# A rope kernel: sin in another PSUM bank than cos, the last tile stored whole, other small transfers between loads and stores

## The chip, the cores and the metric

One core of one Trainium2 chip. The metric is the device time of one execution in microseconds (us). The kernel before takes 162.44 us (median of 3 runs, 162.35 to 162.64). A profiled execution of it has a span of 160.7 us from the first to the last instruction. A profile gives busy times of the engines (PE = TensorE, DVE = VectorE, ACT = ScalarE, POOL = GpSimd, SP = the engine that issues the transfers here), and a record of each DMA packet: start, duration, bytes.

Four terms are used throughout. PSUM is the memory that matmuls write to, divided into banks. A ring is the queue of packets of one of the sixteen DMA engines; it is free when its packets are done. A landing mark is the 4-byte packet that ends a transfer's share on one engine. A packet is in flight from its start to its end. A run counts as slow when it is over 1.5% above the fastest run of the same kernel; ratios use fast runs alone.

## The reference

Rope multiplies the two halves of each head with tables of cosines and sines and adds them crosswise:

```python
x = x.reshape(16, 512, 16, 64)             # batch, seq, heads, head_dim; float32
x1, x2 = x[..., :32], x[..., 32:]
cos, sin = cos[None, :, None, :], sin[None, :, None, :]    # each (512, 32) before
out = concatenate([x1 * cos - x2 * sin, x1 * sin + x2 * cos], axis=-1)
```

x and out are 33.55 MB each. Nothing is read twice, so 67.1 MB have to move.

## The kernel before

The work is cut into eight tiles of 128 partitions x 8 rows of 1024 floats (4 MiB, 32 KB a partition). Five tile buffers are filled ahead; a tile is changed in place and stored from the same buffer. The three places that the change touches:

```python
FIRST = (3, 8)
LAST_OUT = (4, 8)              # rows at which the last tile's stores are cut
EXTRA = (2, 4, 5, 6)           # partitions of the small transfers
...
    load(0, 0, FIRST[0])
    tabs = bp.tile([P, 2 * dim], FP32, name="b")
    nc.sync.dma_start(out=sin_sb, in_=sin_v)
    nc.sync.dma_start(out=cos_sb, in_=cos_v)
    ...                        # the rest of tile 0, then tiles 1 to 4
    spare = fixed.tile([16, len(EXTRA), 16], FP32)
    for i, n in enumerate(EXTRA):
        nc.sync.dma_start(out=spare[:n, i], in_=sin_v[:n, :16])   # read by nobody
...
    tab = pfix.tile([P, BANK], FP32)                   # one PSUM bank
    cos_t = tab[:, : KK * half]
    sin_t = tab[:, KK * half : 2 * KK * half]          # the same bank
    ...
    nc.tensor.matmul(out=sin_t, lhsT=spread, rhs=sin_sb, start=True, stop=True)   # L113
    nc.tensor.matmul(out=cos_t, lhsT=spread, rhs=cos_sb, start=True, stop=True)   # L114
    nc.vector.tensor_scalar_mul(out=sns[:, :, 0, :], in0=sin_k, scalar1=-1.0)     # L116
    nc.vector.tensor_copy(out=sns[:, :, 1, :], in_=sin_k)                         # L117
```

In the loop over tiles, POOL makes x times sin (L165), VectorE makes x times cos in PSUM (L141) and adds the two (L189); for two of eight rows TensorE and ScalarE do the adding. At the end of each tile SP issues its store (L78); after the store of tile 2 it issues the loads of tiles 5 to 7 (L74), each when the store that used its buffer has landed.

## Time and profile before

| what, in the profiled run of before | value |
|---|---|
| span; time of this run | 160.7 us; 162.47 us |
| last landing marks of the sixteen engines start | 158.45 to 159.51 us (mean 158.79) |
| last pair sum of VectorE ends | 148.23 us |
| landing of the last store | 159.85 us |

The prediction below shows the lines that carry this, and puts the span together from the packet records. One view more is needed, the issuer's own part of the timeline (start, duration, engine and line, transfer, count; the duration of a merged row includes the waits between):

```profile
7.26 6.85 SPq L92 DMA_DIRECT2D spare<-in_sin_dram  x4
30.43 34.26 SPq L78 DMA_DIRECT2D out_dram<-xt  x3
64.86 17.66 SPq L74 DMA_DIRECT2D xt<-in_x_dram  x3
82.63 65.97 SPq L78 DMA_DIRECT2D out_dram<-xt  x6
```

```profile
146.11 2.48 SPq L78 DMA_DIRECT2D out_dram<-xt  x2
```

```profile
148.26 0.33 SPq L78 DMA_DIRECT2D out_dram<-xt  x1
```

These are the first answer for the whole span, then two closer looks at its end. The reader is to see that the second half of the last tile is issued at 148.26, when store 6 is just leaving the rings (148.72 to 149.79 by the landing marks). The first half, issued at 146.11, lies in between and keeps the rings full.

### The profile page before, as it was taken

The numbers are of one execution on the slowest core, as the hardware profiler recorded it, in microseconds if no ns is written. First come the engines' busy times: TensorE is split into PE (matmuls) and PEld (weight loads), VectorE is DVE, ScalarE is ACT, GpSimd is POOL, SyncE is SP. The second block draws the span as 40 slices with busy tenths as digits, with TensorE's granted clock in tenths as the row PEclk, the third lists the DMA queues.
The fourth block names the chain that finished last, engine by engine and source line by source line (L and its number), as shares of the span: only waits on it lengthen the run. The fifth ranks groups of instructions, "written<-read, shape, count | busy, mean of one in ns | idle before, by whom it ended". The sixth has DMA issues, their size and how long they took to land.

```text
span 160.7 us, 443 instructions
## 1 busy us (share of the span) xinstructions
PE 60.8 (38%) x71; PEld 19.3 (12%) x71; DVE 136.3 (85%) x85; ACT 18.7 (12%) x25; POOL 127.1 (79%) x38
## 2 busy tenths in 40 slices
PE   3041925056503931192308350664048402932000
PEld 0011301021102210131003010210022001300000
DVE  1059969999999999999999999999999999998000
ACT  0001311003000301012100310031003010211000
POOL 1039999999999999988998899898998899840000
PEclk9999995557655685559555855576556855595555
DMA  5999999999999999999999999999999999999994
GB/s 177 410 408 473 392 514 400 392 473 440 392 449 449 408 400 498 408 392 498 418 392 465 440 400 465 440 400 408 457 432 408 465 424 408 473 416 416 428 412 204
DMA packets 2787, 67.25 MB, mean 419 GB/s; under 512 B 354, under 2 KB 482, under 8 KB 482
## 3 DMA queue, kind: packets, MB, share of 16 engines
q1 hardware_dynamic: 2786, 67.24, 98.0%
q14 instruction: 1, 0.01, 0.0%
HBM read 33.69 MB, written 33.55 MB: 418 GB/s over the span
## 4 chain that ended last, share of the span: by engine, by line
DVE 68%; issue 12%; POOL 6%; DMA 4%; PE 1%; SPq 0%; DVEq 0%
DVE xt L189 33%; DVE pd L141 31%; POOL b L165 6%; DMA b<-in_sin_dram 4%; DVE pe_ps L141 3%; PE tab L113 1%; PE tab L114 1%; DVE sns L116 0%; DVE xt L150 0%; DVE own_ps L141 0%; SPq L74 0%; DVE sns L117 0%; DVEq L189 0%
## 5 line engine op out<-in xcount | busy, mean ns | idle before, releaser
L165 POOL TENSOR_TENSOR b<-xt,sns 128x2048 f32<-128x2048 f32 (+1 forms) x32 | 126.4, 3978 | 14.7 <-DVE sns L117 9.3
L189 DVE TENSOR_TENSOR xt<-pd,b 128x2048 f32<-128x2048 f32 x24 | 54.9, 2286 | 2.4 <-POOL b L165 1.6
L141 DVE TENSOR_TENSOR pd<-xt,tab 128x2048 f32<-128x2048 f32 x24 | 55.0, 2291 | 0.2
L176 PE MATMUL own_ps<-xt,ident 128*128 128x512 f32 x32 | 30.2, 1100 | 54.4 <-DVE xt L150 48.7
L176 PE MATMUL pe_ps<-b,ident 128*128 128x512 f32 x32 | 28.8, 1001 | 24.0 <-DVE pe_ps L141 24.0
L176 PEld LDWEIGHTS own_ps<-xt,ident 128*128 128x128 f32 x32 | 9.4, 323 | 74.3 <-DVE xt L150 59.7
L209 ACT COPY xt<-own_ps 128x1024 f32<-128x1024 f32 x8 | 8.1, 1012 | 73.7 <-PE own_ps L176 73.7
L181 ACT COPY xt<-pe_ps 128x512 f32<-128x512 f32 x16 | 9.4, 585 | 38.2 <-PE pe_ps L176 38.2
L176 PEld LDWEIGHTS pe_ps<-b,ident 128*128 128x128 f32 x32 | 8.4, 290 | 42.8 <-DVE pe_ps L141 34.1
L141 DVE TENSOR_TENSOR pe_ps<-xt,tab 128x512 f32<-128x512 f32 x16 | 11.0, 685 | 0.0
L141 DVE TENSOR_TENSOR own_ps<-xt,tab 128x1024 f32<-128x1024 f32 x8 | 9.8, 1223 | 0.0
L150 DVE TENSOR_TENSOR xt<-xt,tab 128x1024 f32<-128x1024 f32 x8 | 9.7, 1213 | 0.0
L116 DVE TENSOR_SCALAR sns<-tab 128x256 f32<-128x256 f32 x1 | 0.4, 424 | 8.2 <-PE tab L114 8.2
L113 PE MATMUL tab<-b,spread 64*128 64x256 f32 x2 | 1.2, 697 | 5.0 <-DMA b<-in_sin_dram 5.0
L209 ACT ACT_TABLE_LOAD x1 | 1.3, 1283 | 15.4 <-DVE xt L150 15.4
L101 PE MATMUL own_ps<-zero 128*128 128x512 bf16 x2 | 1.0, 618 | 1.2 <-DVE zero L97 1.2
L113 PEld LDWEIGHTS tab<-b,spread 64*128 64x128 f32 x2 | 0.5, 310 | 5.9 <-issue 5.9
L114 PE MATMUL tab<-b,spread 64*128 64x256 f32 x2 | 1.1, 631 | 0.0
L97 DVE MEMSET zero<- 128x256 uint32 x1 | 0.3, 272 | 0.9 <-PEq L240 0.9
L114 PEld LDWEIGHTS tab<-b,spread 64*128 64x128 f32 x2 | 0.7, 334 | 0.2
L101 PE MATMUL pe_ps<-zero 128*128 128x512 bf16 x1 | 0.6, 631 | 0.0
L101 PEld LDWEIGHTS <-zero 128*128 128x128 bf16 x3 | 0.3, 123 | 1.5 <-DVE zero L97 1.2
(9 smaller groups left out, 1.8 us busy)
## 6 DMA issues: line engine op xcount, KB each, us to landing
xt<-in_x_dram SPq DMA_DIRECT2D x7, 4096.0 KB, 29.8
out_dram<-xt SPq DMA_DIRECT2D x7, 4096.0 KB, 24.7
out_dram<-xt SPq DMA_DIRECT2D x2, 2048.0 KB, 10.2
xt<-in_x_dram SPq DMA_DIRECT2D x1, 2560.0 KB
xt<-in_x_dram SPq DMA_DIRECT2D x1, 1536.0 KB
b<-in_sin_dram SPq DMA_DIRECT2D x1, 64.0 KB
b<-in_cos_dram SPq DMA_DIRECT2D x1, 64.0 KB
spare<-in_sin_dram SPq DMA_DIRECT2D x1, 0.1 KB
```

The source lines that it names most:

```text
L97: nc.vector.memset(zero, 0.0)
L101: nc.tensor.matmul(out=ps, lhsT=zero[:, :P], rhs=zero, start=True, stop=True)
L113: nc.tensor.matmul(out=sin_t, lhsT=spread, rhs=sin_sb, start=True, stop=True)
L114: nc.tensor.matmul(out=cos_t, lhsT=spread, rhs=cos_sb, start=True, stop=True)
L116: nc.vector.tensor_scalar_mul(out=sns[:, :, 0, :], in0=sin_k, scalar1=-1.0)
L141: nc.vector.tensor_tensor(out=o, in0=i, in1=cb, op=ALU.mult)
L150: nc.vector.tensor_tensor(out=heads(r), in0=heads(r), in1=s, op=ALU.mult)
L165: nc.gpsimd.tensor_tensor(out=o, in0=i, in1=sb, op=ALU.mult)
L176: nc.tensor.matmul(out=ps, lhsT=ident, rhs=other, start=False, stop=True, skip_group_check=True)
L181: nc.scalar.copy(out=r, in_=pe_ps)
L189: nc.vector.tensor_tensor(out=r, in0=ps, in1=b, op=ALU.add)
L209: nc.scalar.copy(out=r0, in_=own_ps)
```

## The change

The intent: let VectorE's first use of sin start without waiting for cos, so that all computing runs a little earlier; store the last tile with fewer, larger packets, since its store can now be issued early enough; and use less of the small transfers that sit between loads and stores.

```diff
-LAST_OUT = (4, 8)
-
-EXTRA = (2, 4, 5, 6)
+LAST_OUT = (8,)
+
+EXTRA = (1, 1, 1, 1, 3)
@@
-    sin_t = tab[:, KK * half : 2 * KK * half]
+    sin_t = pd.tile([P, 2 * dim], FP32, name="pd")[:, : KK * half]
```

## The prediction

> **What bounds the kernel now.** I read the page's header and the forty slices first, then the DMA queues, then the chain that ended last, then the waits of the DMA queue, and last the packet records of the trace (start, duration and bytes of each packet; they name no DMA engine).
>
> ```profile
> span 160.7 us, 443 instructions
> ...
> DVE  1059969999999999999999999999999999998000
> ...
> DMA  5999999999999999999999999999999999999994
> ...
> q1 hardware_dynamic: 2786, 67.24, 98.0%
> ...
> HBM read 33.69 MB, written 33.55 MB: 418 GB/s over the span
> ...
> DVE 68%; issue 12%; POOL 6%; DMA 4%; PE 1%; SPq 0%; DVEq 0%
> ```
>
> The reader is to see two rows that both look full. VectorE is at 9 almost everywhere, but its last three slices (12 us) are 0; the DMA row is at 9 up to the last slice, and its queue's packets took 98.0% of sixteen engines' span. The chain gives VectorE 68%, because it follows the last instruction back and the last instruction is VectorE's; it doesn't say that a faster VectorE would end the kernel sooner. The 12% of "issue" is the stretch after VectorE has stopped, in which stores drain. A table of stretches says it more sharply:
>
> ```profile
> core 0: us, PE busy (x) PEld busy (x) DVE busy (x) ACT busy (x) POOL busy (x), PEclk, DMA share, GB/s
> ...
> 60.00:100.00 40.00, 15.25 (x18) 4.56 (x16) 39.69 (x24) 4.95 (x7) 37.73 (x11) 0.59 1.00 433
> 100.00:147.00 47.00, 21.27 (x24) 6.37 (x24) 46.52 (x29) 6.55 (x9) 39.69 (x10) 0.61 1.01 432
> ...
> 149.80:158.40 8.60, 0.00 (x0) 0.00 (x0) 0.00 (x0) 0.00 (x0) 0.00 (x0) 0.50 1.00 429
> ```
>
> The DMA share is 1.00 with VectorE busy and with VectorE silent; the rate is the same 429 to 433 GB/s. The packet records agree: a 32 KB packet takes 1.213 us (median of 1792, and the fastest 25% too), a 16 KB packet 0.611 us (256 of them). Sixteen packets are in flight in every microsecond from 3 us to 158 us, but for one at 79 us (15.8). The first packet starts at 1.75 us, and the packets' summed time over 16 is 157.46 us. 1.75 + 157.46 = 159.2 us, and the sixteen last packets end between 158.45 and 159.51 us. So the span is: 1.75 us before the first byte, 157.0 us of solid transfers, 0.7 us in which the engines that ended early wait for the last one (mean end 158.79, last 159.51), and 1.2 us of landing and closing. Nothing that computes is in that sum, provided that the queue never runs dry.
>
> **What the Trainium skill says.** (1) "DMA: Bandwidth & Descriptors", section "Where 436 GB/s comes from": the ceiling of the ports is 435.2 GB/s. The trace agrees: 16 x 32768 B / 1.213 us = 432 GB/s. The same section expects about 358 GB/s for traffic with HBM; here the whole span averages 418, so the measurement decides against that figure. (2) The same page, "Why a DMA increments its semaphore by 16 and not by 1": the number of engines k is the largest up to 16 that divides the slowest dimension that isn't 1, and on this path the lowest-numbered k engines are used. The trace agrees for the small transfers of before: 17 packets of 64 B, which is 2+4+5+6, and 337 of 4 B, which is 20 large transfers x 16 + 17. For a transfer of one partition the slowest dimension that isn't 1 could be the 16 elements, which would make k = 16 with 4 B each; no run here shows it yet. (3) "PSUM — Partial Sum Buffer", section "PSUM bank collisions raise a hardware error": engines must be kept apart by bank, not by address. The trace agrees that VectorE's read of sin waits for the matmul of cos, which writes other columns of the same bank.
>
> ```profile
> 7.68 1.19 PE tab L113 x2
> 8.87 0.87 PE tab L114 x2
> 9.74 0.02 issue
> 9.76 0.42 DVE sns L116
> 10.19 0.34 DVE sns L117
> 10.53 0.07 issue
> 10.60 3.30 POOL b L165
> ```
>
> This is the chain in order of time. L113 spreads sin and is done at 8.87; L114 spreads cos and is done at 9.74; VectorE's first use of sin starts 20 ns after L114, 0.89 us after its own data are there. POOL, which waited 9.3 us for the tables, starts at 10.60.
>
> **The change part by part.** *Sin in another bank.* sin_t moves from columns 256 to 511 of the cos bank to the buffer of the pair products, whose first real use comes later on the same VectorE queue. Removed: the 0.87 us of L114 ahead of L116. Nothing is added. POOL then starts at about 9.73, and because the first pair sum at 21.94 waits for POOL (1.6 us) and VectorE is then back to back, everything that VectorE does after it moves by 0.87: the last pair sum ends at 147.37 instead of 148.23. cos is needed by VectorE only after the two sign copies and the 0.23 us copy, at about 9.95, after L114's 9.74, so it becomes no new wait. What this is worth by itself: the stores of tiles 0 to 6 are issued into a queue that has work for many microseconds (store 0 issued at 30.43 behind loads that end at 51.8; store 6 issued at 132.25, its first packets after 139.0), so 0.0 us. It matters only for the last store.
>
> *Last tile whole.* Before, the two halves are issued at 146.11 and 148.26; store 6 leaves the engines between 148.72 and 149.79. After, one store is issued when the last pair sum ends, at about 147.40. How long from issue to the first packets? The first load has an idle queue: issued at 0.73, sixteen packets in flight between 1.75 and 2.36, so 1.0 to 1.6 us (the page in (2) gives about 0.6 us to the first byte; this case shows 1.0, and I use that). 147.40 + 1.0 to 1.6 = 148.4 to 149.0, against rings that come free from 148.72 to 149.79. So no gap on most engines and at most 0.3 us on the earliest, which end 1 us ahead of the last anyway. Gain: on one engine a tile in whole rows takes 9.681 us (from landing marks at 71.125 and 80.806), in two halves 4.862 + 4.862 = 9.724, so 0.043 us less. The two parts belong together: without the 0.87 us, the packets would come at 149.3 to 149.9 and nearly every engine would idle 0.1 to 0.6 us.
>
> *Small transfers.* They lie between the loads, which end at 51.8, and store 0. Data plus mark take 13 ns of an engine (starts 51.794, 51.802, 51.807). Before, engines 0 and 1 have four, 2 and 3 three, 4 two, 5 one. After, with k as many engines as partitions, engine 0 has five, 1 and 2 one, the others none: +13 ns on engine 0, up to -39 ns on the others. If one partition is cut into sixteen pieces, every engine has four more pairs than engines 6 to 15 have now, +52 ns at most. There are five in place of four, so the rotation of the eight landing semaphores moves by one: store 0 would wait for load 2's landing at about 33.3 rather than go at 29.6, still 18 us before its ring position is reached; the later ones wait for stores that landed 50 us earlier. Nothing on the path.
>
> Sum: 0 - 0.043 + (-0.04 to +0.05) = about -0.04 us, plus luck in the order in which engines end.
>
> **The rivals.** *The last store comes too late.* If the issue of 128 rows under load takes 2 us instead of 1.0 to 1.6, packets come at 149.4 to 150.0, later than every ring is free: end + 0.2 us. For it: nobody waits on an idle ring under load in this trace, so the latency is known from the cold start alone. Against: even then the loss is bounded by a few tenths. If the 0.87 us isn't gained as well, it is up to 1 us, 163.4. *The compute path carries to the end.* If VectorE's chain set the end, 0.87 us would come off: 161.6. Against it: the rings held sixteen packets in flight while VectorE worked, and 10 us of stores follow it. *The engines' order of ending changes.* The spread of the sixteen marks is 0.51 us at 22.6, 0.55 at 61.4, 0.80 at 80.8, 0.86 at 100.2, 1.06 at 110 and stays there; it grows where single packets took 1.25 to 1.62 us (at 50.5, 80.0 and 108.6 to 109.5). Those slow packets belong to no store or load that the change touches. If the new offsets avoid some of them, up to 0.7 us (159.51 to the mean 158.79) could be won; if they add one on the last engine, 0.4 lost. This is the largest uncertain term.
>
> **Range and chances.** Time and span of the profiled run are 162.47 and 160.7, and the three runs lie in 162.35 to 162.64. From 162.44 I take 0.04 by count and another 0.1 because small offsets were presumably chosen for a better order of ending: 162.3 us. The range 161.9 to 162.7 holds the order of ending (some 0.4 either way) and the small late-store rival. A change of 2% is 3.2 us; the removable parts of the span, the 0.7 us of spread and the 0.043, don't reach it, and the worst rival loses 1 us. Faster by over 2%: 0.01; within 2%: 0.98; slower: 0.01.
>
> **What would show it right or wrong.** In the changed profile: VectorE's first use of sin at about 8.9 us, released by L113 (bank step); POOL's first product at about 9.7 and the last pair sum ending at about 147.4 (shift carried); one last store of 4096 KB issued at about 147.4; still about sixteen packets in flight between 148 and 150 us (no gap), and a mean DMA share of 98%; the number of packets under 512 B telling k for one partition (7 small ones, or 64 and 3). Wrong would be a last pair sum still at 148.2, a hole in the DMA row at 148 to 150, or an end that moves by more than 0.5 us without a change in the spread of the last packets.

## The result

Changed kernel: 162.59 us median (162.23 to 162.75, 6 runs). Before, with the runs on the same occasion: 162.54 us (162.27 to 162.85, 6 runs). The ratio is 0.9999, with a 95% interval of 0.9982 to 1.0016. A ratio is the mean time of one kernel's fast runs over that of the other's of the same rounds, so not quite the ratio of the medians quoted. So the change is worth nothing that the runs can tell.

The page of the changed kernel:

```profile
span 160.8 us, 444 instructions
...
DVE  1079979999999999999999999999999999996000
...
DMA  5999999999999999999999999999999999999993
...
q1 hardware_dynamic: 2622, 67.24, 97.9%
...
DVE 67%; issue 12%; DMA 7%; POOL 4%; SPq 1%; DVEq 0%
```

VectorE stops a little earlier (its last busy slice is 6 instead of 8). The DMA row is what it was: 9 throughout, 97.9% of sixteen engines' span instead of 98.0%. There are 164 packets fewer (2622 instead of 2786): 128 data packets and 16 landing marks of the store that was cut in two, and 10 + 10 of the small transfers.

The timeline of the changed kernel at the start:

```profile
7.82 1.19 PE L113 MATMUL pd<-b,spread 64*128 64x256 f32 x2 [5.17 <-DMA b<-in_sin_dram]
...
8.80 1.06 PE L114 MATMUL tab<-b,spread 64*128 64x256 f32 x2
9.04 0.42 DVE L116 TENSOR_SCALAR sns<-pd 128x256 f32<-128x256 f32 x1 [7.49 <-PE pd L113]
9.38 0.41 DVE L117 COPY sns<-pd 128x256 f32<-128x256 f32 x1
9.88 4.51 POOL L165 TENSOR_TENSOR b<-xt,sns 128x2048 f32<-128x2048 f32 x1 [8.57 <-DVE sns L117]
```

The brackets say how long an engine idled and what released it. L116 now starts at 9.04, released by L113 (before: 9.76, released by L114), while the matmul of cos is still running (8.80 + 1.06 = 9.86). POOL starts at 9.88 instead of 10.60. Both moved by 0.72 us and not by 0.87, because sin itself landed later in this execution: L113 starts at 7.82 instead of 7.68.

The end of the changed kernel, VectorE's last instruction and then the issue of the last store, from two looks at the timeline:

```profile
145.21 2.29 DVE L189 TENSOR_TENSOR xt<-pd,b 128x2048 f32<-128x2048 f32 x1
147.56 0.33 SPq L78 DMA_DIRECT2D out_dram<-xt  x1
```

The last pair sum ends at 147.50 instead of 148.23: the 0.73 us of the start have arrived at the end undiminished. The one store of 4096 KB is issued at 147.56. Store 6 leaves the rings between 148.75 and 149.95, and the packets of store 7 follow each mark 5 or 6 ns later; there are 16.0 packets or more in flight in every microsecond from 140 to 158. So all computing ended 0.73 us earlier, and the transfers went on as before. The sixteen last marks lie between 158.43 and 159.63 us, mean 158.75 (before 158.79), last one 0.12 us later than before.

### The profile page after: what moved, and what is told of

Its sections match the earlier page's. It is cut to its first block, busy times and chain, and to the rows that moved or that the text cites. A ratio compares the mean times of both kernels' runs of the same rounds, so it can differ in the third digit from the quotient of the medians.

```text
span 160.8 us, 444 instructions
## 1 busy us (share of the span) xinstructions
PE 55.9 (35%) x71; PEld 18.4 (11%) x71; DVE 136.2 (85%) x85; ACT 18.4 (11%) x25; POOL 127.1 (79%) x38
## 3 DMA queue, kind: packets, MB, share of 16 engines
q1 hardware_dynamic: 2622, 67.24, 97.9%
## 4 chain that ended last, share of the span: by engine, by line
DVE 67%; issue 12%; DMA 7%; POOL 4%; SPq 1%; DVEq 0%
DVE xt L189 33%; DVE pd L141 30%; DMA xt<-in_x_dram 7%; POOL b L165 4%; DVE pe_ps L141 4%; SPq L85 0%; SPq L84 0%; DVE own_ps L141 0%; DVE xt L150 0%; DMA spare<-in_sin_dram 0%; SPq L74 0%; DVEq L189 0%
## 5 line engine op out<-in xcount | busy, mean ns | idle before, releaser
L176 PE MATMUL own_ps<-xt,ident 128*128 128x512 f32 x32 | 29.2, 1068 | 57.0 <-DVE xt L150 52.1
L176 PE MATMUL pe_ps<-b,ident 128*128 128x512 f32 x32 | 24.6, 863 | 25.8 <-DVE pe_ps L141 23.3
L176 PEld LDWEIGHTS pe_ps<-b,ident 128*128 128x128 f32 x32 | 7.5, 260 | 43.4 <-DVE pe_ps L141 35.4
L116 DVE TENSOR_SCALAR sns<-pd 128x256 f32<-128x256 f32 x1 | 0.4, 424 | 7.5 <-PE pd L113 7.5
L113 PE MATMUL pd<-b,spread 64*128 64x256 f32 x2 | 1.2, 696 | 5.2 <-DMA b<-in_sin_dram 5.2
L113 PEld LDWEIGHTS pd<-b,spread 64*128 64x128 f32 x2 | 0.5, 306 | 6.0 <-issue 6.0
L114 PE MATMUL tab<-b,spread 64*128 64x256 f32 x2 | 1.1, 631 | 0.0
L114 PEld LDWEIGHTS tab<-b,spread 64*128 64x128 f32 x2 | 0.7, 333 | 0.2
```

Of the source, the lines that this page charges most:

```text
L176: nc.tensor.matmul(out=ps, lhsT=ident, rhs=other, start=False, stop=True, skip_group_check=True)
```

## The experiments

All runs are of one core; those of one group shared a chip and the runs of the kernel before. Packets in flight and marks are from the packet records. The summary first:

| run | edit | median us (runs) | before, same chip | ratio to before, 95% interval |
|---|---|---|---|---|
| e1_bank | before + sin in its bank | 162.65 (5) | 162.74 | 0.9993, 0.9979 to 1.0007 |
| e2_whole | before + last store whole | 162.77 (6) | 162.74 | 0.9998, 0.9983 to 1.0013 |
| e3_small | before + new small transfers | 162.57 (6) | 162.74 | 0.9992, 0.9974 to 1.0009 |
| e4_none | changed, no small transfers | 162.45 (5) | 162.74 | 0.9983, 0.9970 to 0.9996 |
| e5_late | changed, last store later | 163.34 (4, one of them slow) | 162.34 | 1.0057, 1.0040 to 1.0074 |
| e6_light | changed, less VectorE work | 162.34 (4) | 162.34 | 1.0001, 0.9985 to 1.0018 |
| e7_bytes | changed + 512 KB of load | 163.70 (4) | 162.34 | 1.0088, 1.0070 to 1.0106 |
| e8_eight | changed, eight small transfers | 166.07 (4) | 162.34 | 1.0233, 1.0217 to 1.0248 |
| e9_late2 | e5_late once more | 163.29 (4) | 162.31 | 1.0053, 1.0016 to 1.0089 |
| e10_late4 | changed, still later | 165.83 (4) | 162.31 | 1.0206, 1.0175 to 1.0237 |
| e11_none2 | e4_none once more | 162.30 (6) | 162.31 | 0.9987, 0.9963 to 1.0012 |
| e12_after | changed kernel once more | 162.40 (6) | 162.31 | 0.9994, 0.9968 to 1.0020 |

The theory throughout: sixteen DMA engines, each at a fixed pace, set the end from 1.75 us on, and computing is hidden as long as no ring runs dry. The main rival at first: the parts have effects that cancel.

### The three parts one at a time

e1_bank:

```diff
-    sin_t = tab[:, KK * half : 2 * KK * half]
+    sin_t = pd.tile([P, 2 * dim], FP32, name="pd")[:, : KK * half]
```

> The kernel before with the bank part alone. Theory (the sixteen DMA engines set the end, computing is hidden): last pair sum ends 0.7 to 0.9 us earlier, at about 147.4, sixteen packets in flight as before, time the same as before within 0.2 us. Rival (VectorE's chain carries to the end): 0.7 to 0.9 us faster.

Measured: the same time. The timeline of this run shows that the part worked:

```profile
7.67 1.19 PE L113 MATMUL pd<-b,spread 64*128 64x256 f32 x2 [5.03 <-DMA b<-in_sin_dram]
...
8.90 0.42 DVE L116 TENSOR_SCALAR sns<-pd 128x256 f32<-128x256 f32 x1 [7.35 <-PE pd L113]
...
9.74 4.51 POOL L165 TENSOR_TENSOR b<-xt,sns 128x2048 f32<-128x2048 f32 x1 [8.44 <-DVE sns L117]
```

With sin landing at the same moment as before, L116 moves by 0.86 us (9.76 to 8.90) and the last pair sum ends at 147.38, 0.85 us before that of the kernel before. The time did not follow: 0.85 us would be a ratio of 0.9948, outside the interval. VectorE's chain doesn't set the end.

e2_whole:

```diff
-LAST_OUT = (4, 8)
+LAST_OUT = (8,)
```

> The kernel before with the whole last store alone, which is then issued at about 148.3 instead of 147.6. Theory: packets in 1.0 to 1.2 us for the first engine and up to 1.6 for the last, so rings that come free at 148.7 wait some 0.5 us, the last one (149.8) hardly: last packet 0 to 0.15 us later, time within 0.2 us of before, and a dip below sixteen packets in flight between 148.7 and 149.9. Rival (issue under load takes 2 us): 0.5 to 0.7 us slower. Rival (the two parts of the change cancel, whole store gains): faster by more than 0.2 us.

Measured: the same time. Without the bank part the last store is issued here at 148.09:

```profile
148.09 0.33 SPq L78 DMA_DIRECT2D out_dram<-xt  x1
```

The rings come free from 148.58 on; the first packets of the store start between 148.92 and 149.12 on fourteen of them. The other two, free at 149.43 and 150.20, had theirs waiting. So up to fourteen rings stood idle, for up to 0.34 us, and 11.7 packets were in flight in the half microsecond from 148.5. But the end did not move by that: the ring that came free last, at 150.20, ended last, at 159.88, 9.68 us later. The dip filled time in which the early engines would have waited at the end (marks' spread 1.62 us before the dip, 1.21 us after it). It also measured the term that the prediction had from a cold start only: from issue to packets 0.83 to 1.03 us.

e3_small:

```diff
-EXTRA = (2, 4, 5, 6)
+EXTRA = (1, 1, 1, 1, 3)
```

> The kernel before with the new small transfers alone. Theory: 13 ns of an engine each, time the same within 0.2 us. Store 0 issued at about 33.4 instead of 30.4 because of the shifted semaphore rotation, with no gap in the packets. Rival (offsets of engines matter for the order of ending): spread of the last sixteen packets clearly different from 1.06 us in the direction of the time.

Measured: the same time. Store 0 is issued at 33.38, without a gap in the packets, since the loads end at 51.9. The spread of the last marks is 1.32 us (before 1.06), and the time is not longer for it: the spread is that of one execution, and the times of one kernel differ by 0.6 us among its runs (before: 162.36 to 162.96).

So the parts don't cancel: each by itself does nothing that the runs can tell, within about 0.2%.

### No small transfers

```diff
-    for i, n in enumerate(EXTRA):
-        nc.sync.dma_start(out=spare[:n, i], in_=sin_v[:n, :16])
```

> The changed kernel with no small transfers at all. Theory: 0.01 to 0.07 us less work on engine 0, time the same within 0.2 us, spread of the last packets again 0.8 to 1.2 us, because it grows at single slow packets and not at the small transfers. Rival (the small transfers steer the order of ending): spread below 0.5 us or above 1.6, time moved with it by 0.3 us or more.

Measured: 162.45, ratio 0.9983, just clear of 1, and 0.28 us below before by the ratio: a miss of my 0.2, if a small one. The spread of its last marks was 1.04 us, no other than with the transfers. Since this was a candidate for a better kernel, it ran again beside the changed kernel:

> The changed kernel without small transfers, once more on another occasion, beside the changed kernel itself: it came out at 0.9983 of before, just clear of 1. Theory (chance in the order of ending): within 0.15 us of before and of the changed kernel this time. Rival (a real gain): again 0.2 to 0.3 us faster than both.

> The changed kernel itself, as the partner of the run without small transfers. Theory: within 0.2 us of before; spread of the sixteen last packets 0.8 to 1.5 us as in the other runs.

Measured on another chip: 162.30 without them, 162.40 with them (means 162.29 and 162.40), 162.31 before; the ratio to before is 0.9987 and its interval holds 1. Spreads 0.89 and 1.07 us. Both occasions lean the same way, but the second is not clear of chance: without them it is 0.11 us under the changed kernel, and 0.18 us under before by the means, of which 0.12 us come from one run of before at 163.67. Whether the small transfers cost a tenth of a microsecond stays open; that they gain anything, no run shows.

### Less computing, more bytes

e6_light leaves VectorE's in-place product out (a wrong result):

```diff
-        own_product(r0)
```

> The changed kernel without VectorE's in-place product of the own row (wrong result on purpose): 8 x 1.2 us less on VectorE. Theory: VectorE and all issues of stores run some us ahead, time the same within 0.2 us. Rival (VectorE bounds): 5 to 9 us faster.

Measured: ratio 1.0001 to before. Eight products of 1.21 us are gone, and the last store is issued 4.5 us earlier than in the changed kernel (line from the issuer's timeline):

```profile
143.01 0.33 SPq L78 DMA_DIRECT2D out_dram<-xt  x1
```

It isn't 9.7 us earlier because computing now meets POOL and the loads: in this run POOL waited 3.3 us and VectorE 1.4 us for loads. The time doesn't change.

e7_bytes:

```diff
+    more = fixed.tile([P, dim], FP32)
+    nc.sync.dma_start(out=more, in_=x_v[0][:, :dim])
```

> The changed kernel with one more load of 512 KB into a buffer that nobody reads, queued after the small transfers. Theory: 524288 B / 432 GB/s = 1.21 us slower, 0.75%, with packets in flight at sixteen all along. Rival (the DMA engines have room): no change.

Measured: 163.70 against 162.34, ratio 1.0088, so 1.4 us by the ratio and 1.36 by the medians (expected 1.21; its marks' mean ends at 159.99, 1.24 us after the 158.75 of the changed kernel's first profile). Taking away ten microseconds of VectorE's work gives nothing; adding 0.8% of bytes costs 0.9% of time. That is what a bound looks like from both sides. The queue's line of this run, packets, MB and share of sixteen engines' span, shows that the engines stayed as full as before:

```profile
q1 hardware_dynamic: 2766, 67.77, 98.1%
```

The 128 added packets of 4 KB took 0.161 us each (median), 1.31 us an engine, which is a little more than 1.21 at the pace of the 32 KB packets.

### How late may the last store be?

e5_late (and the same kernel again as e9_late2) puts two products that nobody reads ahead of the last pair sum; e10_late4 puts four:

```diff
+        if t + 1 == NT:
+            for _ in range(2):          # e10_late4: range(4)
+                cos_product(own_ps, rows(t, ROW_OWN), ROW_OWN)
         pair_sum(*p1, b1)
```

> The changed kernel with two more 128x1024 products on VectorE (to a buffer that nobody reads any more) ahead of the last pair sum: the last store is issued some 2.3 us later, at about 149.85. Theory: the rings are free from 148.7 to 150.0, packets come 1.0 to 1.6 us after the issue, at 150.9 to 151.5, last packet at about 161.1: 1.2 to 1.6 us slower than the changed kernel, with a hole in the DMA row near 150. Rival (the compute chain never matters within a few us): no change. Rival (VectorE's chain sets the end already): 2.3 us slower.

Measured: three of four runs at 163.16 to 163.36 us (ratio of the fast runs 1.0057), about 1.0 us over before, a miss of my 1.2 to 1.6. The fourth run, the one that was profiled, took 192.13 us and counts as slow:

```profile
L176 PE MATMUL pe_ps<-b,ident 128*128 128x512 f32 x32 | 55.9, 1868 | 11.2 <-DVE pe_ps L141 11.2
L176 PE MATMUL own_ps<-xt,ident 128*128 128x512 f32 x32 | 55.5, 1976 | 43.5 <-DVE xt L150 38.6 <-issue 5.0
```

These are groups of instructions (busy us, mean ns of one). TensorE's matmuls took 1.87 and 1.98 us there, against 0.86 and 1.07 us in the changed kernel's profile, VectorE then waited 3.5 us a tile for ScalarE, and the rings ran dry. Why TensorE was slow in that one execution, the profile doesn't show (it gives a granted clock of 1.0, and 0.64 for the changed kernel's, so a lower clock it was not). Nothing about the change is concluded from it. So the same kernel ran again:

> The same kernel as in the run with two more VectorE products ahead of the last pair sum, once more, since that run's profile fell in a slow state. The whole store alone showed 0.83 to 1.03 us from issue to packets on rings that stand idle. With that: issue at about 149.8, packets at 150.6 to 150.9, last packet at about 160.5, some 0.9 us slower than the changed kernel, an idle stretch of all sixteen between about 149.9 and 150.6. Rival (latency of 1.0 to 1.6 us as in the prediction): 1.2 to 1.6 us.

> Four more products in place of two, so 2.3 us more on VectorE before the last store. Theory (once the rings have run dry, the last store's issue sets the end, microsecond for microsecond): 2.2 to 2.4 us slower than with two, 3.1 to 3.3 us slower than the changed kernel. Rival (part of the delay is still hidden): clearly under 2 us more than with two.

Measured: 163.29 and 165.83 us; the changed kernel on the same chip 162.40. Two products cost 0.9 us, as expected, and four 3.4 us, 2.54 more than two: a little over the 2.2 to 2.4 and 3.1 to 3.3 expected. The profiles give the reason. The issues of the last store, first with two products, then with four:

```profile
149.28 0.33 SPq L78 DMA_DIRECT2D out_dram<-xt  x1
```

```profile
152.09 0.33 SPq L78 DMA_DIRECT2D out_dram<-xt  x1
```

The stretches around it, with four products:

```profile
core 0: us, PE busy (x) PEld busy (x) DVE busy (x) ACT busy (x) POOL busy (x), PEclk, DMA share, GB/s
...
148.40:149.90 1.50, 0.00 (x0) 0.00 (x0) 1.47 (x3) 0.00 (x0) 0.00 (x0) 0.50 0.06 22
149.90:152.60 2.70, 0.00 (x0) 0.00 (x0) 2.12 (x1) 0.00 (x0) 0.00 (x0) 0.50 0.00 0
152.60:154.00 1.40, 0.00 (x0) 0.00 (x0) 0.00 (x0) 0.00 (x0) 0.00 (x0) 0.50 0.87 374
```

The next to last number is the DMA share: VectorE is at work for 2.12 us of a stretch in which no DMA engine has anything to do (a packet counts where it starts, so 0.06 in the line above is the tail of packets that began before). The packets start at 150.11 to 150.26 and at 152.92 to 153.06, in both cases 0.83 us after the issue for the first and 0.97 to 0.98 for the last engine. Between the two runs the issue moves by 2.81 us and the last mark by 2.80 us (160.01 to 162.82): once the rings are dry, the issue of the last store sets the end, microsecond for microsecond. That was the theory; the rival, that part of the delay stays hidden, is out. Of the 2.81 us, 2.5 are the two products more (I had put 2.3), and the rest is that sin's matmul (L113) began 0.27 us later in the second of these executions. In the first, the issue came at 149.28 and not at 149.8 as expected; that run was the fastest of its four (163.00).

With 0.83 us, measured on idle rings, the changed kernel's margin can be estimated: its last store is issued at 147.56, so packets are there from 148.39, and the first ring comes free at 148.75. It had 0.36 us to spare before any engine would wait, and over 1 us before the last one would (149.95 less 147.56 + 1.03).

### Eight small transfers

```diff
-EXTRA = (1, 1, 1, 1, 3)
+EXTRA = (1,) * 8
```

> The changed kernel with eight small transfers of one partition in place of five. They cost 13 ns each, but the eighth takes the landing semaphore of load 4, the last load of the first group, and the DMA queue's issuer waits for it until about 52.8; store 0 is issued after that, at about 53. Theory: the rings, which end the loads and small transfers at 51.9 to 52.3, get store 0 only at about 54, so all sixteen stand still for about 1.8 us: 1.5 to 2.2 us slower. Rival (only bytes and packets count): the same within 0.2 us.

Measured: 166.07 us, ratio 1.0233: slower by over 2%, and about twice what I expected. The gap is there as expected, in the issuer's timeline and in the stretches:

```profile
7.03 45.66 SPq L92 DMA_DIRECT2D spare<-in_sin_dram  x8
52.82 10.84 SPq L78 DMA_DIRECT2D out_dram<-xt  x3
```

```profile
core 0: us, PE busy (x) PEld busy (x) DVE busy (x) ACT busy (x) POOL busy (x), PEclk, DMA share, GB/s
...
51.50:52.00 0.50, 0.50 (x2) 0.34 (x1) 0.50 (x2) 0.00 (x0) 0.50 (x1) 0.50 0.04 1
52.00:53.50 1.50, 1.50 (x3) 0.42 (x2) 1.50 (x2) 0.00 (x0) 1.50 (x2) 0.50 0.00 0
```

The eighth small transfer holds the issuer until 52.8, and store 0, finished by VectorE 23 us before, goes out behind it. The rings are empty from 52.0 to about 53.7, and each stands idle for 2.0 us on average. Three small transfers more cost that. What I had not expected is a further 1.5 us: the packets' summed time over 16 is 158.86 us against 157.35 in the changed kernel. After the gap 74 packets of 32 KB take over 1.24 us, 29 us too long in all; the changed kernel has 11 such packets with 1.3 us. Fifteen of the 74 follow the restart directly, but they make up only 0.5 us. The loss lies in 54 packets of up to 2.31 us at 78 to 85 and at 110 to 113 us, where stores and loads take turns. The mean of the last marks is 3.52 us later, which is 2.0 of gap and 1.5 of slow packets.

Why those packets are slow is open. My reading was that engines in step disturb one another, since all sixteen start within 0.2 us of each other after the gap. Step alone is not enough: in e9_late2 and e10_late4 all sixteen restart within 0.15 us of each other for the last store, and none of its packets takes over 1.26 us. Nor does it seem to be needed: the slow profile of e5_late has 27 such packets, 14 us too long, at 112 to 116 us, with marks 1.04 us apart just before.

## Why the prediction was right

**The bound.** Right. The span was put together from 1.75 us of start, transfers without a gap, the last engine's lateness and the landing, and neither 0.85 us less on the compute path (e1_bank) nor 4.5 us (e6_light) moved the time, while 0.8% more bytes did (e7_bytes). Which part of the way, the engines, the ports or the memory, sets the 1.213 us of a 32 KB packet, no run here separates.

**The bank part.** Right: L116 waits for L113 alone, POOL and VectorE run earlier by that much to the very end, 0.85 us where sin landed at the same moment, 0.73 in the changed kernel's profile. The sum gave it 0.0 us of time, and that is what e1_bank measured within its interval. Behind it stood another limit close by: in the changed kernel the chain goes back from POOL's second product, at 14.37 us, to transfers (tile 0's second part, until 13.95, and a small one) and no longer to sin. It costs nothing yet, as POOL's first product ends only then. Three readings in the prediction were wrong without changing its result. The 12% of "issue" are not the stretch after VectorE has stopped: they are 19.0 us of short pieces between VectorE's instructions (0.44 and 0.98 us, again and again), and the chain ends with VectorE at 148.23. Cos does become a new wait: the 0.23 us copy (L119) writes into the cos bank, and in e1_bank it starts at 9.76, just after L114's end at 9.72 and 0.1 us after L117's end (in e5_late, where TensorE was slow, the waits name L114 for it, with 0.9 us); VectorE waits 1.5 us for POOL later, so nothing comes of it. And the pair sum at 21.94 is the second one; the first, at 15.29, doesn't wait.

**The last tile whole.** The 0.043 us are there on each ring: from mark to mark a ring takes 9.681 us for the whole tile (148.746 to 158.427), as computed. The mean of the last marks went from 158.79 to 158.75, which agrees with the sum of 0.04, but in two profiles of the changed kernel it differs by 0.14 us (158.75 and 158.61 in e12_after), so that is no proof. One term was mis-sized: 1.0 to 1.6 us from issue to packets, taken from the cold start, is 0.83 to 1.03 us on idle rings in the middle of the kernel (e2_whole, e9_late2, e10_late4). The conclusion drawn from it, no gap with the bank part and a small one without it, held with room to spare. The loss that the rival put on the missing bank part, up to 1 us, did not come: e2_whole lost nothing.

**The small transfers.** Right in size (no difference seen in e3_small), and the packets settle the open point: 7 packets of 64 B and 311 of 4 B = 19 large transfers x 16 + 7, so a transfer of one partition goes to one engine and is not cut into sixteen. The turn of the semaphores by one, said to be harmless, was: store 0 at 33.48. e8_eight shows how near the harm lies.

**The rivals.** "The compute path carries to the end" is out by e1_bank and e6_light. "The last store comes too late" did not happen, but is real: e9_late2 has it. "The order of ending changes" is what was left: the last mark came 0.12 us later though the mean came earlier, and the last marks' spread was 0.89 to 1.44 us over the fast runs in which the rings had work until the last store, with nothing in the edits to match (0.15 us in e9_late2 and e10_late4, where all rings restart together). The other 0.1 us that I took off for a better order was a guess and is not borne out: the means of changed and before differ by 0.01%. The time itself, 162.59 us, came out 0.3 us above the 162.3 predicted and 0.1 us inside the range. That the time would stay the same followed from the bound; the 0.04 us of the sum is too small for the runs to confirm.

## What to carry to other kernels

When the DMA row is full from the first slice to the last, put the span together from first packet, packets' time over the number of engines, and the last engine's lateness: what isn't a term of this sum won't change the time, as long as no ring runs dry (e8_eight, e9_late2 and e10_late4 show what happens when one does). A part of a change that is worth nothing by itself can still keep another from doing harm: the earlier VectorE kept the rings full under the whole last store, though here neither the dip without it nor the 0.04 us shows in the time. And count the transfers in flight, not only their bytes: one that needs a semaphore still in use stops its issuer, and everything behind it.

## What the Trainium skill lacked or had wrong

- "DMA: Bandwidth & Descriptors", "Where 436 GB/s comes from": for traffic between HBM and SBUF it lets the HBM side bind at about 358 GB/s, without a condition. With loads and stores mixed and one core at work, the runs show 418 GB/s over the span and 432 to 434 in its middle, near the 435.2 that the section gives for the ports. The page isn't wrong as a whole: its section "Measured (HBM→SBUF, 128 partitions, SWDGE, issued from GpSimd)" keeps the 358 for two cores that stream at once and has 425 GB/s for one core alone. No run here has two cores.
- The same page, "Latency and other measured facts": about 600 ns to the first byte on this path; it doesn't say from when it counts. The runs show 0.83 us from the start of the issue to the first packet on idle rings in three runs (0.97 to 1.03 us until the last idle ring has one), and 1.0 us at the start of the kernel. From the end of the issuing instruction (0.33 and 0.38 us) it is 0.50 and 0.64 us, so the runs don't contradict the page.
- The same page, "Why a DMA increments its semaphore by 16 and not by 1": it goes by the dimensions as the instruction carries them, and doesn't say that a contiguous row of 16 floats is carried as a single element. The trace of the changed kernel has these transfers as dst_num_elem=[1,1], dst_elem_size=64, and shows k = 1: one packet of 64 B and one mark each.
- No page that I looked up says what a transfer costs that reuses a landing semaphore still in use: the issuer stood until 52.8 us, each ring stood idle for 2.0 us, and 166.07 us came of it, slow packets included.
- No page that I looked up says that packets can get slower long after a gap in the rings: in e8_eight 54 packets took up to 2.31 us in place of 1.213, at 78 to 113 us after a gap at 53, and cost 1.5 us per engine. The cause is open.
